# One transpose of a two-part staging tile becomes two, and the value matmuls take the high parts first

## The chip, the cores and the metric

The kernel runs on one core of one Trainium2 chip. The metric is the device time of one execution in microseconds. The engines are PE (matrix products; its weight loads are shown apart as PEld), DVE (vector), ACT (scalar), POOL (GpSimd) and SP (which here only issues DMA transfers).

## The reference, cut to what matters

A streaming-encoder block on x of 2048 rows by 1024 columns, float32. RMSNorm and one projection give the queries, keys and values of two kinds of heads; their outputs are normed, joined and projected back; a SwiGLU feed-forward part with a second RMSNorm follows. The change lies in the two attentions:

```python
# differential attention, 4 heads of value width 128, two softmax maps each
p = jax.nn.softmax(logits, axis=-1)
attn = p[:, :, 0] - lam * p[:, :, 1]
return jnp.einsum('bhqk,bkhd->bqhd', attn, v)
...
# stick-breaking attention, 8 heads of value width 64, strictly causal
log_1mb = jnp.where(mask, jax.nn.log_sigmoid(-z), 0.0)
rem = lax.cumsum(log_1mb, axis=3, reverse=True) - log_1mb
a = jnp.where(mask, jnp.exp(jax.nn.log_sigmoid(z) + rem), 0.0)
return jnp.einsum('bhqk,bkhd->bqhd', a, v)
```

Both are causal (the first by chunks of 64 rows), so a query block of 128 rows meets only the key blocks up to its own.

## The kernel before, in words

**Precision.** Every float32 operand of a matrix product is held as two float16 parts, a high one (the value rounded) and a low one (what is left). A product is made of three float16 products: high by high, high by low, low by high.

**Work and its order.** There are eight head groups g. Groups 0 to 3 hold one differential head each (`diff_attn`), groups 4 to 7 two stick-breaking heads each (`sb_attn`). While the attention of group g runs, the projection of group g+1 is woven in (`advance`, `proj_stream`), and out-projection work at the end. The feed-forward part comes after it all, from about 1360 us on. A scheduler of the framework places the instructions of each engine's queue at build time, by a timeline that it simulates and by priorities given in the code; the hardware then runs each queue strictly in that order, each instruction waiting for its semaphores.

**A unit of attention.** For a query block i (16 of them), a map or head m, and a stretch b of at most 1024 keys, the probabilities form a tile of 128 queries by n keys, n from 128 to 1024. In groups 0 to 3 the two maps are combined first, so that there are 24 units a group; in groups 4 to 7 there are 48. That makes 4 x 24 + 4 x 48 = 288 units. `split_t` (line 449) takes such a float32 tile and does three things:

- `to16` (line 454, instruction line 89 on ACT or DVE, 93 on POOL) casts it to the high part, in the first n columns of a staging tile s16. In stick-breaking heads ACT always does this.
- `tt` (line 455, instruction line 98) subtracts and writes the low part to the next n columns. In stick-breaking heads POOL always does this.
- `SP.dma_start_transpose` (line 460) turns all 2n columns, by DMA, into aT: up to 16 blocks of 128 keys by 128 queries, the high ones first.

The staging tile has three buffers and aT six (`SB`, `AB`, line 39); in groups 4 and 5 some units borrow buffers of the projection's tiles instead (lines 450 to 457). In a trace the staging tile is called `s`.

**Values.** `pv` (line 512) multiplies the n/128 blocks with the values and adds up in PSUM (yp): for each block j three matmuls, high aT by high v, high aT by low v, low aT by high v. In differential heads it runs two query blocks after the probabilities (`held`, line 584), in stick-breaking heads five or seven units after them (`lag`, line 599), and it may be placed only after the scores of the newest unit (line 632).

**SP's queue.** One queue issues nearly all transfers, in order: the transposes of line 460 and those of the queries and keys (line 409), copies of query halves (411), loads of normed rows for the projection (xt, 423), weights (271), stores of the attention's output (ms, 496). Each waits in the queue for its data, its buffer, and a completion semaphore out of eight that are used in turn.

Of the kernel before, what the change touches and what calls it, by code (L numbers as in the profile page):

```python
# [16 lines left out]
ALU = mybir.AluOpType  # L17
# [4 lines left out]
S, D, P = 2048, 1024, 128  # L22
# [37 lines left out]
def block(tc, a, out):  # L60
    nc = tc.nc
    PE, ACT, DVE, POOL, SP = nc.tensor, nc.scalar, nc.vector, nc.gpsimd, nc.sync
    top = ExitStack()
    with top:
# [11 lines left out]
        def pick(**cost):  # L76
            e = min(cost, key=lambda k: load[k] + cost[k] * KW[k])
            load[e] += cost[e] * KW[e]
            return e
# [5 lines left out]
        def to16(dst, src, n, engines="ADP", psum=False):  # L85
            cost = {"A": 0.84 * n + 110, "D": (1.05 if psum else 0.53) * n + 70, "P": 1.1 * n + 80}
            e = pick(**{k: cost[k] for k in engines})
            if e == "A":
                ACT.copy(dst, src)  # L89
            elif e == "D":  # L90
                DVE.tensor_copy(dst, src)
            else:
                POOL.tensor_scalar(dst, src, 1.0, 0.0, op0=ALU.mult, op1=ALU.add)

        def tt(dst, a_, b_, op, n, engines="DP"):
            cost = {"D": 1.15 * n + 70, "P": 2.45 * n + 80}
            e = pick(**{k: cost[k] for k in engines})
            (DVE if e == "D" else POOL).tensor_tensor(dst, a_, b_, op)  # L98

        def pri(k):  # L100
            def deco(f):
                @functools.wraps(f)
                def g(*args):
                    with tc.high_priority(PRI[k]) if PRI[k] else nullcontext():
                        return f(*args)
                return g
            return deco

        def nm(s):
            uid[0] += 1  # L110
            return f"{s}{uid[0]}"
# [144 lines left out]
        with ExitStack() as ph1:  # L256
# [75 lines left out]
            @pri("pm")  # L332
            def proj_turned(G, xt, pq, pv, r):
                xv = xt[:].rearrange("p (s k n) -> p s k n", s=2, k=KT)
                for c in range(3):
                    n = 0
                    for kt in range(KT):
                        for xi, wi in ((0, 0), (0, 1), (1, 0)):
                            w_, x_ = G["w"][:, wi, kt, 128 * c : 128 * c + 128], xv[:, xi, kt, :]
                            o = pv[:, P * r : P * r + P] if c == 2 else pq[:, 256 * c + P * r : 256 * c + P * r + P]  # L340
                            PE.matmul(o, lhsT=x_ if c == 2 else w_, rhs=w_ if c == 2 else x_, start=n == 0, stop=n == 23)  # L341
                            n += 1

            @pri("po")
            def turned_out(pq, pv, qT, kT, v, j):
                two = slice(j - 1, j + 1)
                q2, k2 = (pq[:, 256 * c : 256 * c + 256].rearrange("p (t n) -> p t n", t=2) for c in range(2))
                for m in range(2):
                    ACT.mul(qT[:, m, two, :], q2, half[:, m : m + 1])
                    DVE.scalar_tensor_tensor(qT[:, 2 + m, two, :], q2, half[:, m : m + 1], qT[:, m, two, :], op0=ALU.mult, op1=ALU.subtract)  # L350
                note("A", 800)
                note("D", 800)
                split_psum(kT[:, 0, two, :], kT[:, 1, two, :], k2, 256)
                vv = v[:, two, :].rearrange("p t (h s e) -> p t h s e", h=2, s=2)
                split_psum(vv[:, :, :, 0, :], vv[:, :, :, 1, :], pv[:, :256].rearrange("p (t h e) -> p t h e", t=2, h=2), 256)
# [92 lines left out]
            @pri("spl")  # L448
            def split_t(src, n, he="ADP", le="DP", wide=None):
                if wide is not None and wide % 5 in (1, 3):  # L450
                    s16 = pp.tile([P, 4, 256], F32, tag="raw", name=nm("s16"))[:].rearrange("p t n -> p (t n)").bitcast(F16)
                else:
                    s16 = s16p.tile([P, 2048], F16, tag="s16", bufs=SB, name=nm("s16"))
                to16(s16[:, :n], src, n, he)
                tt(s16[:, n : 2 * n], src, s16[:, :n], ALU.subtract, n, le)
                if wide is not None and wide % 4 == 3:
                    aT = pp.tile([P, 4, 4, 2, 64], F16, tag="st", name=nm("aT"))[:].rearrange("p c t s e -> p (c t) (s e)")
                else:
                    aT = sp.tile([P, 16, P], F16, tag="aT", bufs=AB, name=nm("aT"))
                SP.dma_start_transpose(aT[:, : 2 * n // P, :], s16[:, : 2 * n])  # L460
                return aT

            @pri("fin")
# [47 lines left out]
            @pri("pv")  # L511
            def pv(G, yp, y0, aT, b, n, o, wd, start, stop):
                nb = n // P
                for j in range(nb):
                    v = G["v"][2 * b + j // 4][:, j % 4, :]
                    for q, (a_, v_) in enumerate(((j, o), (j, o + wd), (nb + j, o))):
                        PE.matmul(yp[:, y0 : y0 + wd], lhsT=aT[:, a_, :], rhs=v[:, v_ : v_ + wd], start=start and j == 0 and q == 0, stop=stop and j == nb - 1 and q == 2, skip_group_check=True)  # L517

            def diff_attn(g, G):
                @pri("at")  # L520
                def probs(i):
# [43 lines left out]
                    for (b, n, z0), (_, _, z1) in zip(*zs):  # L565
                        DVE.scalar_tensor_tensor(z0[:, :n], z1[:, :n], rc[:], z0[:, :n], op0=ALU.mult, op1=ALU.add)
                        note("D", 1.05 * n + 130)
                        aTs.append((b, n, split_t(z0[:, :n], n)))
# [5 lines left out]
                def values(i, aTs, ssum):  # L574
                    r, k = fq(g, i)
                    if r == 0:
                        ypd[0] = ps.tile([P, 512], F32, tag="yp", name=nm("yp"))
                    yp = ypd[0]
                    for q, (b, n, aT) in enumerate(aTs):
                        pv(G, yp, P * r, aT, b, n, 0, 128, r == 0 and q == 0, r == k - 1 and q == len(aTs) - 1)  # L580
                    if r == k - 1:
                        finish(g, G, i, k, yp, ssum)
# [12 lines left out]
            def sb_attn(g, G):  # L595
# [5 lines left out]
                @pri("at")  # L601
                def stage_a(i, m, b):
                    L = (i + 1) * 128
                    n = min(1024, L - 1024 * b)
                    be, om = z4(), z4()
                    if b == i // 8:
                        DVE.memset(om[:, n : n + 1], 8192.0)
                    else:
                        DVE.tensor_copy(om[:, n : n + 1], last[m][:, 0:1])
                    last[m] = om  # L610
                    for c in range((n - 1) // 512, -1, -1):
                        lo, hi = 512 * c, min(512 * c + 512, n)
                        w = hi - lo
                        sc = ps.tile([P, 512], F32, tag="sc", bufs=4, name=nm("sc"))
                        front.append(score_chunk(G, sc, i, 2 * b + c, m, w // P, b == i // 8 and hi == n, turned(g)))
                        aside = c == 1 and turned(g)
                        beta = be[:, lo:hi] if aside else sc[:, :w]
                        ACT.activation(om[:, lo:hi], sc[:, :w], AF.Sigmoid, scale=G["nkz"][:])  # L618
                        ACT.activation(beta, sc[:, :w], AF.Sigmoid, scale=G["kz"][:])  # L619
                        ov = om[:, lo:hi][:, ::-1]  # L620
                        DVE.tensor_tensor_scan(ov, ov, sc[:, :w], om[:, hi : hi + 1], op0=ALU.mult, op1=ALU.bypass)  # L621
                        (POOL if aside else DVE).tensor_tensor(be[:, lo:hi], beta, om[:, lo + 1 : hi + 1], ALU.mult)  # L622
                        note("A", 1.7 * w + 400)
                        note("D", 2.1 * w + 150)
                        note("P" if aside else "D", (1.65 if aside else 1.05) * w + 100)
                    wide[0] += 1
                    return n, split_t(be[:, :n], n, "A", "P", wide[0] if g < NG - 2 else None)
# [670 lines left out]
```

## Time and profile before

| | us |
|---|---|
| median of 3 runs | 2703.69 |
| lowest and highest | 2701.29, 2709.12 |
| profiled execution | 2702.93 |
| its span (first to last instruction) | 2701.0 |

The profile is one execution. "Busy" counts an engine's own instructions; waiting, branching and issuing DMAs is the sequencer's and is not counted. A queue of an engine's sequencer is written with a q (SPq). A group's row gives the line, engine, operation, what is written <- what is read, the count, then busy us and mean ns of one, then the engine's idle time just before them and what ended it. A wait's row gives who waited for what: us in total, times, longest.

The attention with its projections takes the first half of the span, the feed-forward part the second:

| stage | about | what runs |
|---|---|---|
| differential heads | 100 to 600 us | groups 0 to 3, projections of 1 to 4 |
| stick-breaking heads | 600 to 1360 us | groups 4 to 7, projections of 5 to 7, out-projection |
| feed-forward | 1360 to 2701 us | nothing that the diff touches |

### The profile page before, as it was taken

To read this page: it belongs to the slowest core of one execution; us is meant where nothing else is said; L and a number is where in the kernel's file an instruction comes from. 1 tells how busy PE (TensorE), PEld (TensorE's weight loads), DVE (VectorE), ACT (ScalarE), POOL (GpSimd) and SP (SyncE) were. 2 spreads that over 40 slices of the span, in tenths; PEclk is the share of its full clock that TensorE was granted. 3 is DMA by queue.
4 is the path that set the end of the run, shared out by engine and by line. 5 is a ranking of instruction groups with operands and counts; after the bars stand their busy time and mean duration, and the time that the engine had idled before them with its cause. 6 is when DMAs were issued, how large, how long until landed. Compare 5 with 4: busy or idle time off the path is not lost. (4 is left out here: it accounts for less than half of the span.)

```text
span 2701.0 us, 50505 instructions
## 1 busy us (share of the span) xinstructions
PE 2508.6 (93%) x19628; PEld 1507.6 (56%) x19628; DVE 1959.8 (73%) x3712; ACT 1344.7 (50%) x2487; POOL 1517.8 (56%) x1097
## 2 busy tenths in 40 slices
PE   7998989899988989889999999999999999999999
PEld 4655656577776776567774444444444444444444
DVE  6898879899989889887866877778685543433434
ACT  4665656567978878765634534435352112111121
POOL 2578767768767767545665755665564332322323
PEclk9999999999999999999999999999999999999999
DMA  6778697768989989997996566565748744635532
GB/s 221 211 163 184 143 200 172 172 145 183 195 175 185 178 166 206 208 205 203 230 317 232 211 232 219 207 239 183 253 171 330 304 159 157 234 132 184 202 110 94
DMA packets 619584, 534.40 MB, mean 198 GB/s; under 512 B 480640, under 2 KB 548224, under 8 KB 609104
## 3 DMA queue, kind: packets, MB, share of 16 engines
q1 hardware_dynamic: 617520, 529.09, 70.1%
q8 instruction: 154, 2.52, 0.4%
q0 software_dynamic: 512, 1.36, 0.2%
q14 instruction: 86, 0.70, 0.1%
q10 hardware_dynamic: 1312, 0.72, 0.1%
HBM read 261.08 MB, written 147.32 MB: 151 GB/s over the span
## 5 line engine op out<-in xcount | busy, mean ns | idle before, releaser
L98 POOL TENSOR_TENSOR s<-z,s 128x1024 f16<-128x1024 f32 (+7 forms) x288 | 471.5, 1646 | 141.8 <-ACT s L89 118.2
L506 PE MATMUL sc<-kT,qT 128*128 128x512 f16 (+3 forms) x1520 | 382.7, 354 | 51.1 <-DVE z L622 18.6
L1104 PE MATMUL pd<-wd,act 128*128 128x512 f16 x1764 | 392.8, 380 | 5.3 <-DVE cu L1038 4.7
L621 DVE TENSOR_TENSOR_SCAN z<-z,sc 128x512 f32<-128x512 f32 (+3 forms) x320 | 352.8, 1112 | 56.5 <-ACT sc L619 34.6
L325 PE MATMUL pj<-w,xt 128*128 128x384 f16 x1920 | 354.6, 333 | 17.1 <-ACT raw L374 5.8
L1004 PEld LDWEIGHTS <-wu 128*128 128x128 f16 x1848 | 181.9, 98 | 224.6 <-issue 12.8
L1004 PEld LDWEIGHTS <-wg 128*128 128x128 f16 x1848 | 181.3, 98 | 222.9 <-issue 9.3
L517 PE MATMUL yp<-v,aT 128*128 128x64 f16 (+1 forms) x4896 | 271.2, 205 | 36.9 <-DMA aT<-s 35.7
L517 PEld LDWEIGHTS <-aT 128*128 128x128 f16 x4896 | 239.1, 100 | 114.4 <-DMA aT<-s 46.7
L98 POOL TENSOR_TENSOR act<-cg,act 128x512 f16<-128x512 f32 x109 | 150.7, 1393 | 259.4 <-ACT act L1063 259.4
L1104 PEld LDWEIGHTS <-act 128*128 128x128 f16 x1764 | 172.9, 98 | 213.5 <-issue 7.2
L325 PEld LDWEIGHTS <-xt 128*128 128x128 f16 x1920 | 187.8, 99 | 147.2 <-issue 23.4
L89 ACT CAST s<-z 128x128 f16<-128x128 f32 (+7 forms) x215 | 173.3, 810 | 135.9 <-DMA aT<-s 44.6
L98 POOL TENSOR_TENSOR stages<-stages 128x512 f32<-128x512 f32 x97 | 171.4, 1767 | 116.5 <-DVE wg L220 42.2
L618 ACT ACTIVATE z<-sc,c 128x512 f32<-128x512 f32 (+3 forms) x320 | 211.2, 665 | 24.4 <-PE sc L506 12.4
L98 POOL TENSOR_TENSOR hs<-hs,cu 128x512 f32<-128x512 f32 x102 | 133.6, 1317 | 159.3 <-DVE hs L1110 59.7
L506 PEld LDWEIGHTS <-qT 128*128 128x128 f16 x1520 | 128.8, 99 | 119.7 <-issue 23.9
L831 PE MATMUL po<-wo,mt 128*128 128x256 f16 x1536 | 182.4, 279 | 12.6 <-DVE xf L834 8.6
L1063 ACT CAST act<-cg 128x512 f16<-128x512 f32 x126 | 76.7, 616 | 231.1 <-DVE cg L1069 192.7
L1110 DVE SCALAR_TENSOR_TENSOR hs<-pd,c,hs 128x512 f32<-128x512 f32 x144 | 106.0, 747 | 115.0 <-PE pd L1104 105.3
L341 PE MATMUL pj<-xt,w 128*128 128x128 f16 x2304 | 177.4, 222 | 6.2 <-DVE v L363 5.2
L1004 PE MATMUL pm<-X,wu 128*128 128x512 f16 x792 | 179.8, 381 | 2.1 <-ACT cg L1049 1.7
(254 smaller groups left out, 4812.3 us busy)
## 6 DMA issues: line engine op xcount, KB each, us to landing
xt<-xs SPq DMA_DIRECT2D x112, 512.0 KB, 4.5
hs<-hd SPq DMA_DIRECT2D x72, 512.0 KB, 4.5
hd<-hs SPq DMA_DIRECT2D x56, 512.0 KB, 5.9
split<-wg SPq DMA_DIRECT2D x11, 1792.0 KB, 6.9
split<-wu SPq DMA_DIRECT2D x11, 1792.0 KB, 6.7
split<-wd SPq DMA_DIRECT2D x11, 1792.0 KB, 6.8
wg<-split SPq DMA_DIRECT2D x11, 1792.0 KB, 7.5
wd<-split SPq DMA_DIRECT2D x11, 1792.0 KB, 9.0
```

The source lines that it names most:

```text
L89: ACT.copy(dst, src)
L98: (DVE if e == "D" else POOL).tensor_tensor(dst, a_, b_, op)
L325: PE.matmul(pj[:, :384], lhsT=xv[:, xi, kt, :], rhs=G["w"][:, wi, kt, :], start=n == 0, stop=n == 23)
L341: PE.matmul(o, lhsT=x_ if c == 2 else w_, rhs=w_ if c == 2 else x_, start=n == 0, stop=n == 23)
L506: last = PE.matmul(sc[:, : 128 * w].rearrange("p (t n) -> p t n", n=P), lhsT=G["q"][i // 4][:, a_, i % 4, :], rhs=G["k"][q][:, b_, 0:w, :] ...
L517: PE.matmul(yp[:, y0 : y0 + wd], lhsT=aT[:, a_, :], rhs=v[:, v_ : v_ + wd], start=start and j == 0 and q == 0, stop=stop and j == nb - 1 a ...
L618: ACT.activation(om[:, lo:hi], sc[:, :w], AF.Sigmoid, scale=G["nkz"][:])
L621: DVE.tensor_tensor_scan(ov, ov, sc[:, :w], om[:, hi : hi + 1], op0=ALU.mult, op1=ALU.bypass)
L831: PE.matmul(po[:, sl], lhsT=mt[:, kt, P * xi : P * xi + P], rhs=wos[2 * h + n][wi][:, kt, :], start=q == 0, stop=q == 23)
L1004: PE.matmul(ps_[:].rearrange("p (t n) -> p t n", n=P), lhsT=wv[:, wo, wi, 128 * kt : 128 * kt + 128], rhs=X[xo][:, :, xi, kt, :], start=st ...
L1104: PE.matmul(po[:], lhsT=act[:, ao, xi, 128 * j : 128 * j + 128], rhs=W["d"][:, wo, wi, :], start=start and u == 0 and q == 0, stop=u == nu ...
L1110: DVE.scalar_tensor_tensor(dst, po[:], kd[:], src, op0=ALU.mult, op1=ALU.add)
```

## The change

In `split_t` aT is taken ahead of the cast, and the single transpose of 2n columns becomes two of n columns: the high part's right after the cast, the low part's after the subtraction. In `pv` the order of the 3n/128 matmuls of a unit changes: all blocks' high-aT pairs first, then all low-aT ones. Numbers of matmuls, casts and subtractions, their shapes and the bytes moved stay the same; there are 288 more DMA transposes.

```diff
-                to16(s16[:, :n], src, n, he)
-                tt(s16[:, n : 2 * n], src, s16[:, :n], ALU.subtract, n, le)
                 if wide is not None and wide % 4 == 3:
                     aT = pp.tile([P, 4, 4, 2, 64], F16, tag="st", name=nm("aT"))[:].rearrange("p c t s e -> p (c t) (s e)")
                 else:
                     aT = sp.tile([P, 16, P], F16, tag="aT", bufs=AB, name=nm("aT"))
-                SP.dma_start_transpose(aT[:, : 2 * n // P, :], s16[:, : 2 * n])
+                to16(s16[:, :n], src, n, he)
+                SP.dma_start_transpose(aT[:, : n // P, :], s16[:, :n])
+                tt(s16[:, n : 2 * n], src, s16[:, :n], ALU.subtract, n, le)
+                SP.dma_start_transpose(aT[:, n // P : 2 * n // P, :], s16[:, n : 2 * n])
                 return aT
...
             def pv(G, yp, y0, aT, b, n, o, wd, start, stop):
                 nb = n // P
-                for j in range(nb):
+                todo = [(j, a_, v_) for part in (((0, o), (0, o + wd)), ((nb, o),)) for j in range(nb) for a_, v_ in part]
+                for q, (j, a_, v_) in enumerate(todo):
                     v = G["v"][2 * b + j // 4][:, j % 4, :]
-                    for q, (a_, v_) in enumerate(((j, o), (j, o + wd), (nb + j, o))):
-                        PE.matmul(yp[:, y0 : y0 + wd], lhsT=aT[:, a_, :], rhs=v[:, v_ : v_ + wd], start=start and j == 0 and q == 0, stop=stop and j == nb - 1 and q == 2, skip_group_check=True)
+                    PE.matmul(yp[:, y0 : y0 + wd], lhsT=aT[:, a_ + j, :], rhs=v[:, v_ : v_ + wd], start=start and q == 0, stop=stop and q == 3 * nb - 1, skip_group_check=True)
```

## The prediction

> **What bounds the kernel now.** I read the page's busy shares first, then the stretches of the attention stage, then the DMA-issuing queue SP, because the change touches only how the staging tiles of attention are transposed. The page:
>
> ```profile
> PE 2508.6 (93%) x19628; PEld 1507.6 (56%) x19628; DVE 1959.8 (73%) x3712; ACT 1344.7 (50%) x2487; POOL 1517.8 (56%) x1097
> ...
> L517 PE MATMUL yp<-v,aT 128*128 128x64 f16 (+1 forms) x4896 | 271.2, 205 | 36.9 <-DMA aT<-s 35.7
> L517 PEld LDWEIGHTS <-aT 128*128 128x128 f16 x4896 | 239.1, 100 | 114.4 <-DMA aT<-s 46.7
> ```
>
> PE is busy for 93% of the span, and the matmuls that the change reorders (line 517) leave it idle for 36.9 us in all, 35.7 of them until a transposed tile aT lands. PEld shows the same waits from the weight load's side, so the two are not added. Where the attention runs, the stretches (start:end, length, then busy time of PE, PEld, DVE, ACT, POOL, granted clock, DMA share, GB/s) say:
>
> ```profile
> 100.00:600.00 500.00, 456.58 (x3861) 302.41 (x3860) 433.48 (x1284) 302.40 (x791) 351.87 (x252) 0.97 0.76 171
> 600.00:800.00 200.00, 179.93 (x2765) 147.81 (x2763) 181.08 (x336) 167.05 (x318) 147.89 (x114) 0.98 0.94 186
> 800.00:1100.00 300.00, 267.20 (x3858) 205.62 (x3857) 271.58 (x470) 245.40 (x441) 215.38 (x157) 0.98 0.93 187
> ...
> 1200.00:1360.00 160.00, 147.67 (x1599) 124.62 (x1597) 122.92 (x183) 97.61 (x163) 101.68 (x67) 0.98 0.84 214
> ```
>
> From 100 to 600 us (differential heads) PE leads and the DMA engines have a quarter of their time free. From 600 to 1100 (stick-breaking heads) PE 90%, DVE 90%, ACT 83% and the DMA engines 93 to 94% are all nearly full: no engine has room there. After 1360 us nothing of the change runs; the 1340 us of the feed-forward part stay as they are.
>
> The transposes, as the view of line 460 gives them (ns in the SP queue min/median/max; then issue to landing), with the subtraction ahead of them from the view of the staging tile:
>
> ```profile
> L460 SPq DMA_TRANSPOSE aT<-s x288: 1167/1556/5872, 113.7 to 1358.9; - x144
> DMA to landing us min/median/max: 2.3/3.9/7.9
> ```
> ```profile
> L98 POOL TENSOR_TENSOR s<-z,s x288: 416/1890/3642, 112.9 to 1356.1; 128x1024 f16<-128x1024 f32 x70, 128x128 f16<-128x128 f32 x12, 128x640 f16<-128x640 f32 x12, 128x896 f16<-128x896 f32 x12
> ```
>
> One transpose holds SP's in-order queue for at least 1.17 us, whatever its size; ordinary transfers hold it far less (0.53 us for an xt load in the rows below). 288 at the median are 288 x 1.56 = 449 us of SP's time between 114 and 1359 us.
>
> **The change part by part.** Matmuls and weight loads: 4896 of each before and after, the same operands, so no price in PE time. Each aT block still serves two matmuls in a row, then one. ACT, DVE and POOL run the same casts and subtractions. The same bytes are moved.
>
> *Issues.* SP issues 288 transposes more. A half has one to eight 128-column blocks. The small end is the first unit of the attention (two blocks), in SP's timeline; the large end has a row of its own, since the transposes of qT and kT (line 409) are just eight blocks:
>
> ```profile
> 113.67 1.20 SPq L460 DMA_TRANSPOSE aT<-s  x1
> ...
> 118.93 0.53 SPq L423 DMA_DIRECT2D xt<-xs  x1
> ```
> ```profile
> L409 SPq DMA_TRANSPOSE qT<-st x20: 1231/1258/2072, 71.9 to 1177.2; - x20
> L409 SPq DMA_TRANSPOSE kT<-st x20: 1232/1298/3267, 74.0 to 1178.4; - x20
> ...
> DMA to landing us min/median/max: 3.1/3.3/6.6
> ```
>
> So a half costs 1.20 to 1.26 us of SP, a pair 2.40 to 2.52 us. 288 more issues at 1.2 us are 346 us of SP's time. The Trainium skill, "DMA: Bandwidth & Descriptors", section on the anatomy of one DMA, puts nearly all of a DMA's fixed cost of about 2 us (measured there for GpSimd's queue) into the completion and about 50 ns into the sequencer's dispatch; by that the 288 issues would be an estimated 14 us of SP. The trace's 1.17 us minimum, on SP's queue and for a transpose, speaks against it here.
>
> *What covers them.* SP's own waits ahead of line 460 (us in total, times, longest):
>
> ```profile
> SPq L460 <- POOL s L98: 299.3, 123, 11.6
> ...
> SPq L460 <- POOL z L622: 97.4, 39, 9.1
> ...
> SPq L460 <- POOL raw L98: 24.1, 6, 7.3
> ...
> SPq L460 <- POOL s L93: 20.1, 10, 3.8
> ...
> SPq L460 <- POOL yrs L485: 15.4, 8, 3.4
> ```
>
> For 123+39+6+10+8 = 186 of the 288 units SP sat idle, 456 us in all, until GpSimd had ended the low half or what stands just ahead of it. There the high half's issue falls into the wait and costs nothing, as it was meant. About 102 units had no such wait; SP was behind already. Two stretches of SP's timeline show these bursts:
>
> ```profile
> 620.96 15.98 SPq L460 DMA_TRANSPOSE aT<-s  x10
> ...
> 666.99 18.38 SPq L460 DMA_TRANSPOSE aT<-s  x8
> ```
>
> Ten units took 1.60 us each with nothing between them, mostly small ones at the start of a head; eight took 2.30 us each, half of them sixteen blocks long, in a stretch where the DMA engines are 94% busy, so that SP probably waited for room in them. As pairs they take 2.40 to 2.52 us: 0.8 us more a unit in the first kind, 0.2 us in the second. Over 102 units that is 20 to 82 us by which SP falls further behind; I take the middle, 50 us.
>
> *Who waits for that.* SP is one queue. Behind a low half that waits for GpSimd stand the next unit's high half, the xt loads of the projection and the stores of ms; in the built order the two halves of a unit mostly stand side by side, so the high half of unit n+1 cannot pass the low half of unit n. A late landing reaches PE (which runs seven units behind the scores, so some is absorbed) and ACT (which needs the staging buffer back; there are three, and two shared ones in two groups). Whole span, then from 600 to 1200 us:
>
> ```profile
> ACT s L89 <- DMA aT<-s: 44.6, 23, 4.3
> ...
> PE yp L517 <- DMA aT<-s: 35.7, 27, 3.3
> ```
> ```profile
> PE yp L517 <- DMA aT<-s: 13.2, 13, 2.1
> ```
> ```profile
> ACT s L89 <- DMA aT<-s: 24.3, 17, 3.0
> ```
>
> Both engines wait on these landings already, in the stretch in which neither has room, so lateness is not free. I let half of the 50 us through, 25 us (bounds: nothing, and all 82). The high half also needs its aT buffer about 1.9 us (the median subtraction) sooner; with six buffers I price that at nothing, and where a buffer is late it is part of the same lateness, at most 1.9 us a time.
>
> *What is gained.* The last landing of a unit is now that of eight blocks or fewer: 3.3 us after its issue instead of 3.9, so 0.6 us sooner where SP is on time. Outside 600 to 1200 us PE waits 27-13 = 14 times, 22.5 us: 14 x 0.6 = 8 us saved. Inside, SP's lateness eats it.
>
> *Order.* The built program places the value matmuls earlier: at the 128th unit 339 fewer projection matmuls stand ahead of them than before, over units 96 to 192 about 50 to 120. PE passes 2765 matmuls in the 200 us from 600 on, 0.072 us each, so up to 24 us of filler work comes later exactly where SP and the DMA engines are full. The work itself is not lost; I take nothing, and 24 us for the upper end.
>
> *Sum.* 25 - 8 = 17, about +18 us with the rounding of the halves. The profiled execution lasted 2702.9 us (span 2701.0), 0.8 below the median of 2703.7. So 2721 on the profile's own time and **2722** as a median, 0.7% slower.
>
> **The rivals.** Line 460 once more, from 600 to 800 us and from 800 to 1100 us (first row of one, both rows of the other):
>
> ```profile
> L460 SPq DMA_TRANSPOSE aT<-s x66: 1190/1559/5872, 601.0 to 799.7; - x66
> ```
> ```profile
> L460 SPq DMA_TRANSPOSE aT<-s x84: 1167/1630/5492, 799.7 to 1097.4; - x84
> DMA to landing us min/median/max: 2.3/4.5/7.9
> ```
>
> *Halves land earlier, and SP keeps up (faster).* For it: 186 units with an idle SP ahead of them, and a DMA queue with a quarter of its time free before 600 us. Against it: SP's 1.2 us a piece. If SP's lateness stays hidden, each of PE's 27 waits shrinks by 0.6 us (all rows) to 1.2 us (if a full unit's landing of about 4.5 us becomes 3.3): 16 to 32 us, 2672 to 2688, middle 2680. It holds as long as a pair is issued faster than units are made: a unit takes 200 us / 66 = 3.0 us from 600 to 800, a pair 2.5 us and the other transfers some 0.3 (an xt load of 0.53 us to two units). The Trainium skill's rule on dispatch would give this outcome.
> *No change.* From 600 to 1100 us the DMA engines are 93% busy with the same bytes; if they set the pace, the split is hidden and gain and lateness cancel: 2696 to 2711.
> *The split does not do what it says (far slower).* If a high half regularly queues behind a low half that waits for GpSimd, nothing starts earlier and each unit has 1.2 us more of latency, while xt loads stand in the same line. Then all 82 us of lateness come through with the 24 of the order: 2703.7 + 106, about 2810. It decides once the pair plus other transfers (2.8 us) exceeds the unit's 3.0 us by any extra wait of 0.2 us.
>
> **How the numbers follow.** Forecast, moderately slower (2712, where no change ends, to 2778, when all 82 us of lateness come through less the 8 gained): 0.50. Faster: 0.27. No change: 0.15. Far slower: 0.08. A measurement of this kernel tells about 0.3% (8 us) from no change, so faster 0.27, same 0.15, slower 0.58. The range runs from 2672, the low end of the faster rival, to 2778; only the far-slower rival is outside, and some of the tails. The likeliest case alone spans 2712 to 2778.
>
> **What would show it.** SP's view of the two transpose lines should have 288 rows each with minima near 1.17 us and medians of 1.25 to 1.5 us. In bursts, SP's timeline should show pairs at 2.4 to 2.5 us with no gap. The forecast is right if PE's and ACT's waits on aT between 600 and 1200 us grow from 13.2 and 24.3 us to some 20 to 30 more in sum, and PE's waits before 600 us shrink. It is wrong, towards faster, if those waits fall everywhere while SP's waits for GpSimd shrink by about 300 us; wrong towards far slower if xt loads start to hold up PE's projections (lines 325 and 341). A much shorter issue for a half (0.6 us, half of now) would take away the ground of the whole forecast.

## The result and the profile after

The changed kernel takes 2829.99 us (median of 4 runs, 2828.66 to 2834.37) against 2702.49 us: ratio 1.047, 95% interval 1.0456 to 1.0484. It is 127 us slower. The forecast had the sign and was far too small; the time lies above its whole range.

The profiled execution has a span of 2832.5 us. Its page, with the rows that answer to those of before:

```profile
PE 2531.9 (89%) x19628; PEld 1519.7 (54%) x19628; DVE 1960.2 (69%) x3712; ACT 1349.1 (48%) x2487; POOL 1514.8 (53%) x1097
...
L518 PE MATMUL yp<-v,aT 128*128 128x64 f16 (+1 forms) x4896 | 286.8, 206 | 84.2 <-DMA aT<-s 83.8
L518 PEld LDWEIGHTS <-aT 128*128 128x128 f16 x4896 | 248.0, 101 | 164.0 <-DMA aT<-s 103.5
```

The engines do the same work in a longer time: DVE's busy time is 1960 us as before, at 69% of the span and no longer 73%. PE's idle time ahead of the value matmuls went from 36.9 to 84.2 us, and its busy time from 2508.6 to 2531.9 us for the same matmuls; its mean granted clock was 0.967 and no longer 0.98. The stretches (busy time of PE, PEld, DVE, ACT, POOL, granted clock, DMA share, GB/s) show where:

```profile
100.00:600.00 500.00, 435.76 (x3509) 284.00 (x3508) 398.90 (x1197) 285.16 (x744) 333.22 (x238) 0.96 0.74 162
600.00:800.00 200.00, 154.14 (x2105) 121.10 (x2104) 161.86 (x330) 143.71 (x280) 129.34 (x97) 0.93 0.77 154
800.00:1100.00 300.00, 251.71 (x3940) 207.83 (x3939) 239.00 (x422) 215.26 (x395) 185.38 (x142) 0.97 0.84 157
```

From 100 to 600 us PE gets through 3509 matmuls instead of 3861, from 600 to 800 through 2105 instead of 2765. Every engine has room there, and so have the DMA engines, 77% and no longer 94%: everybody waits. The two transposes of a unit (ns in SP's queue, first and last start, landing):

```profile
L459 SPq DMA_TRANSPOSE aT<-s x288: 1103/1236/3911, 114.5 to 1475.3; - x144
...
DMA to landing us min/median/max: 2.3/3.3/10.3
```
```profile
L461 SPq DMA_TRANSPOSE aT<-s x288: 1093/1237/3547, 117.3 to 1479.1; - x144
...
DMA to landing us min/median/max: 2.2/3.0/9.3
```

Each half holds SP for 1.24 us at the median, as forecast. The last one starts at 1479 us; the last transpose of before started at 1359. The two profiled executions differ by 131 us, so 120 of these were lost ahead of that point, in the attention. Some 12 us come behind the last value matmul: 1348 us from there to the end against 1336 before. SP's queue in a stretch of the attention:

```profile
759.33 1.30 SPq L461 DMA_TRANSPOSE aT<-s  x1
760.73 1.27 SPq L459 DMA_TRANSPOSE aT<-s  x1
762.10 1.27 SPq L461 DMA_TRANSPOSE aT<-s  x1
763.47 1.22 SPq L459 DMA_TRANSPOSE aT<-s  x1
...
787.28 2.62 SPq L423 DMA_DIRECT2D xt<-xs  x3
```

In the first rows issue follows issue at 0.1 us, and the three xt loads stand behind them. A stretch of the same queue before has gaps of 1.3 and 2.0 us between the end of one row and the start of the next:

```profile
719.91 0.32 SPq L423 DMA_DIRECT2D xt<-xs  x1
720.32 1.53 SPq L460 DMA_TRANSPOSE aT<-s  x1
723.19 0.32 SPq L423 DMA_DIRECT2D xt<-xs  x1
725.52 9.60 SPq L460 DMA_TRANSPOSE aT<-s  x4
```

Over the whole attention 85 of the 288 transposes of before had a gap of at least 1.2 us ahead of them; in the changed kernel 35 of the 576 have one.

PE's own account, from 100 us to about the last value matmul (same columns as above, first the kernel before, then the changed one):

```profile
100.00:1360.00 1260.00, 1133.51 (x12869) 835.66 (x12868) 1089.67 (x2435) 877.93 (x1843) 862.72 (x624) 0.97 0.85 185
```
```profile
100.00:1480.00 1380.00, 1162.93 (x12897) 851.42 (x12895) 1085.64 (x2435) 883.49 (x1846) 864.73 (x625) 0.95 0.80 169
```

Of the 120 us PE spends 91 idle (217 us and no longer 126) and 29 on nearly the same matmuls at a lower granted clock. Its waits grew from 35.7 to 83.8 us for aT, from 9.7 to 42.5 us for all other transfers, which stand in SP's queue too, and from 71 to 83 us for DVE. How much of the 29 us would be lost without the waits, no run shows.

### The profile page after: what moved, and what is told of

It reads as the page before. It is cut to its first block, busy times and chain, and to the rows that moved or that the text cites. A ratio compares the mean times of both kernels' runs of the same rounds, so it can differ in the third digit from the quotient of the medians.

```text
span 2832.5 us, 51199 instructions
## 1 busy us (share of the span) xinstructions
PE 2531.9 (89%) x19628; PEld 1519.7 (54%) x19628; DVE 1960.2 (69%) x3712; ACT 1349.1 (48%) x2487; POOL 1514.8 (53%) x1097
## 5 line engine op out<-in xcount | busy, mean ns | idle before, releaser
L98 POOL TENSOR_TENSOR s<-z,s 128x1024 f16<-128x1024 f32 (+7 forms) x288 | 461.5, 1609 | 204.3 <-ACT s L89 195.4
L518 PE MATMUL yp<-v,aT 128*128 128x64 f16 (+1 forms) x4896 | 286.8, 206 | 84.2 <-DMA aT<-s 83.8
L518 PEld LDWEIGHTS <-aT 128*128 128x128 f16 x4896 | 248.0, 101 | 164.0 <-DMA aT<-s 103.5
L619 ACT ACTIVATE z<-sc,c 128x512 f32<-128x512 f32 (+3 forms) x320 | 208.4, 655 | 59.1 <-PE sc L509 42.5
L543 DVE TENSOR_SCALAR_CACHE_REDUCE z<-sc,c 128x512 f32<-128x512 f32 (+3 forms) x256 | 162.3, 648 | 44.3 <-PE sc L507 40.0
```

Source lines behind the costliest of these rows:

```text
L518: PE.matmul(yp[:, y0 : y0 + wd], lhsT=aT[:, a_ + j, :], rhs=v[:, v_ : v_ + wd], start=start and q == 0, stop=stop and q == 3 * nb - 1, ski ...
L543: DVE.tensor_scalar(z[:, lo : lo + f], sc[:, :f], kz_d[:], None, op0=ALU.mult, op1=ALU.max, accum_out=mx[:, m, nx : nx + 1])
```

## The experiments

Two things change on the chip: SP issues 288 transposes more (theory A), and the scheduler, which sees other dependencies, puts the instructions of all engines into another order (theory B). To part them, most kernels below have their queues fixed: an ordering edge, which orders issue and makes nobody wait for completion, ties every instruction to the one ahead of it in a given order.

```python
for a_, b_ in zip(at, at[1:]):          # at: the positions of one engine's queue in the given order
    tc.add_manual_dep(ins[b_], ins[a_].name, dep, reason="order")
```

"Old order" is the queue order of the kernel before, "new order" that of the changed kernel. The kernel before gave 2703 to 2705 us beside these runs.

**1. The change in the old order** (`split_old_order`): the changed kernel plus the edges.

> The changed kernel's instructions (two transposes a unit, the high half right after the cast, high blocks first in the values), but every engine's queue is fixed to the order that the kernel before has, with the two transposes side by side where the one stood. Theory A (SP's queue: 288 more issues of about 1.2 us in a queue that runs in order) expects nearly the whole loss without the scheduler's new order: 2780 to 2830 us. Theory B (the scheduler, which takes the halves to be cheaper, built an order that the hardware cannot keep) expects 2690 to 2720 us. If both take part, something between.

2780.0 us, ratio 1.028 (1.0268 to 1.0301): 77 us slower, the lower end of what theory A expected. The extra issues cost that in the order of before; the new matmul order, which is in this kernel too, costs nothing (trial 7). SP's timeline shows the backlog: high (459) and low halves (461) without a gap.

```profile
716.26 1.66 SPq L461 DMA_TRANSPOSE aT<-s  x1
718.01 0.53 SPq L423 DMA_DIRECT2D xt<-xs  x1
718.63 1.18 SPq L459 DMA_TRANSPOSE aT<-s  x1
719.90 1.21 SPq L461 DMA_TRANSPOSE aT<-s  x1
```

Summed over all its transfers between 600 and 1200 us, SP is issuing for 87% of the time; before it was 66%. Who pays, from 600 to 1200 us (us in total, times, longest):

```profile
PE yp L518 <- DMA aT<-s: 44.7, 49, 5.3
```
```profile
ACT s L89 <- DMA aT<-s: 66.6, 33, 7.2
```

Before these were 13.2 and 24.3 us. ACT's wait is the longer: its cast waits for a staging buffer that the late transpose has not read yet. The wait runs from the queue back to the producer.

**2. One transpose in the new order** (`one_new_order`): the kernel before with the new values' order, and edges for the new order.

> One transpose a unit as before, but every engine's queue is fixed to the order of the changed kernel, high blocks first in the values; the one transpose stands where the high half stood. Theory A expects the time of before or some 10 us more, 2695 to 2715 us, since 288 issues are gone. Theory B expects most of the loss, 2780 to 2830 us. The place at the high half makes SP wait for the subtraction there, so a result between is no clean verdict.

2855.1 us, ratio 1.056 (1.0545 to 1.0576). Slower than the change itself, with half its transposes. This does not measure the order cleanly: the values' high matmuls stand early in that order, and here they wait for a transpose that needs both halves (PE waits 97.8 us for aT over the span; 83.8 in the changed kernel). Trial 9 mends most of it.

**3. Both halves issued late, old order** (`split_late_old_order`):

```diff
-                SP.dma_start_transpose(aT[:, : n // P, :], s16[:, :n])
                 tt(s16[:, n : 2 * n], src, s16[:, :n], ALU.subtract, n, le)
+                SP.dma_start_transpose(aT[:, : n // P, :], s16[:, :n])
```

> As the changed kernel in the order of before, but both halves' transposes are issued only after the subtraction, so nothing starts early. If the early high half is worth what it was meant to be (about 2 us of latency a unit), this is 10 to 40 us slower than the same with the early half; if SP's issue time alone counts, within 10 us of it; if a high half that waits in the queue blocks others, this is faster by 5 us or more.

2780.9 us against 2780.0 of trial 1. But the edit did not bring what the expectation says. The subtraction writes other columns than the high half's transpose reads, so neither waits for the other, and the place of a line in the code is not its place in a fixed queue. In the two traces SP's queue holds the same operations in the same order, and PE's too, and in both some 60 of the 288 high halves start before their unit's subtraction has ended. So this is a repeat of trial 1; what the early start is worth it does not show.

**4. The values' order alone, scheduler free** (`pv_only`): the hunk of `pv` without that of `split_t`.

> One transpose a unit as before; only the value matmuls take all high blocks first; the scheduler is free. Theory A expects no change beyond the scheduler's own scatter, 2690 to 2715 us. A theory that the new matmul order itself costs time (theory C) expects 2760 us or more.

2729.8 us, ratio 1.0094 (1.0077 to 1.0111): 27 us, for the same instructions and transfers. Neither theory had expected that: it lies above the range of A and below that of C.

**5. Split only where SP had a gap, old order** (`split_idle_old_order`): here and in 6, 8, 10 and 12 the values keep their old matmul order.

```diff
+                two = next(seen) in TWO
+                if two:
+                    SP.dma_start_transpose(aT[:, : n // P, :], s16[:, :n])
                 tt(s16[:, n : 2 * n], src, s16[:, :n], ALU.subtract, n, le)
+                f = n if two else 0
+                SP.dma_start_transpose(aT[:, f // P : 2 * n // P, :], s16[:, f : 2 * n])
```

> Queues fixed to the order of before, values in the old matmul order; only those 85 units are split before which SP's queue had been empty for at least 1.2 us in the trace of before (the gap between the end of one issue and the start of the next). Theory A (an extra issue costs only where SP has no gap) expects 2690 to 2712 us. If every extra issue costs the same, 77 us / 288 = 0.27 us each, it gives 2726 us.

2702.9 us beside 2704.9, ratio 0.9992 (0.9982 to 1.0002). 85 issues more, free, and no gain clear of noise either: at the lower end of the interval 5 us. Here 83 of the 85 high halves do start before their subtraction has ended, by 1.8 us at the median. This is as near as any variant came to beating the kernel before.

**6. The complement, old order** (`split_busy_old_order`): `TWO` holds the other 203 units.

> The complement: the other 203 units are split, those where SP was busy or nearly so. Theory A expects nearly the whole loss of the fixed order, 2760 to 2785 us. Equal cost for each issue gives 2703 + 203 x 0.27 = 2757 us. If the units with gaps were what holds up the queue, it stays below 2730 us.

2776.1 us, ratio 1.0267 (1.0247 to 1.0287): 71 us, 0.35 us for each of these units. The same kernel with all 288 units split is trial 8, 81 us slower. So most of the loss sits in these units, and the cost depends on where the issue falls. Whether the other 85 are still free once these 203 are split is not shown: 10 us lie between the two trials, and their intervals just overlap.

**7. The values' order alone, old order** (`pv_old_order`).

> One transpose a unit, values with all high blocks first, every queue fixed to the order of before. If the 27 us of the values' order alone came from the scheduler's new order, this is 2700 to 2710 us. If the matmul order itself costs PE time, it is 2720 to 2735 us.

2702.6 us, ratio 1.0001 (0.9985 to 1.0018). So the 27 us of trial 4 are the scheduler's order alone; the new matmul order costs nothing.

**8. The split alone, old order** (`split_only_old_order`): trial 1 without the hunk of `pv`.

> Two transposes a unit, values in the old matmul order (each block's high and low part side by side, so the first block needs both halves), queues fixed to the order of before. If taking high blocks first lets PE start earlier to any use, this is slower than 2780 us by 10 us or more; if the matmul order does not matter, 2775 to 2785 us.

2785.9 us, ratio 1.0304 (1.0277 to 1.033). Trial 1 gave 2780.0 beside a slightly faster kernel before (77 us slower against 81), so taking the high blocks first is worth some 4 us if anything; the two intervals overlap.

**9. One transpose in the new order, at the low half's place** (`one_new_order_low`).

> A fairer trial of the changed kernel's order without its extra issues: queues fixed to the order of the changed kernel, one transpose a unit, standing at the low half's place for 234 units (the other 54 at the high half's place, where the low place would close a circle of waits), and the values of a unit all together at the place of its first low block. If the loss beyond the 77 us of the issues comes from the order, this is 2740 us or more; if the order is harmless and the trial before it was slow for its odd places, 2695 to 2715 us.

2813.2 us, ratio 1.0411 (1.0395 to 1.0428): 110 us slower with as many transposes as before. Its stretches look like those of the change:

```profile
100.00:600.00 500.00, 436.18 (x3563) 286.73 (x3561) 397.54 (x1199) 288.06 (x752) 337.53 (x240) 0.95 0.71 163
600.00:800.00 200.00, 163.10 (x2186) 127.27 (x2184) 171.90 (x342) 151.76 (x290) 137.08 (x102) 0.91 0.74 158
```

PE again passes only 3563 and 2186 matmuls, and no engine nor the DMA engines are full. PE's waits from 600 to 1200 us:

```profile
PE yp L517 <- DMA aT<-s: 17.7, 9, 4.4
PE sc L506 <- DVE z L621: 15.5, 16, 5.1
PE pj L341 <- DVE v L363: 13.2, 6, 4.1
PE sc L506 <- DVE z L622: 9.6, 14, 1.5
```

Here PE waits less for transposes than for DVE to free the scores' and projections' buffers. Over the whole attention its waits for DVE grew from 71 us before to 105, those for aT from 36 to 56. That the queues' orders fit each other less well is the likely reading, not a shown one. 54 of the 288 transposes stand at a place of their own, so the 110 us have a share of that in them.

**10. Three transposes a unit, old order** (`three_old_order`): trial 8 with the low half cut once more.

```diff
-                SP.dma_start_transpose(aT[:, n // P : 2 * n // P, :], s16[:, n : 2 * n])
+                f = n + n // P // 2 * P
+                if f > n:
+                    SP.dma_start_transpose(aT[:, n // P : f // P, :], s16[:, n:f])
+                SP.dma_start_transpose(aT[:, f // P : 2 * n // P, :], s16[:, f : 2 * n])
```

> The suspected cost doubled: queues fixed to the order of before, values in the old matmul order, and three transposes a unit (the low half is cut once more; the 24 units of one block keep two), 264 issues more than with two. With three, SP needs 552 x 1.2 + 288 x 1.2 = 1010 us for these transposes and some 230 us for the rest, about the whole attention stage of 1260 us of before, so theory A expects it to be the bound throughout: each further issue costs nearly its full 1.2 us, 2780 + 264 x 0.8 to 1.2 = 2990 to 3100 us. If the loss with two came from contention of the DMA engines or the order of work, it stays below 2850 us.

2996.4 us, ratio 1.1087 (1.1066 to 1.1109). Against the 2785.9 of trial 8 that is 210.5 us for 264 issues, 0.80 us each: more than twice the 0.27 to 0.35 us of the second issue. The dose is steep because the cover is used up: SP is issuing for 91% of the time from 600 to 1200 us, and its gaps ahead of these transposes sum to 90 us (127 in trial 8, 292 before). The DMA engines meanwhile have more and more room:

```profile
600.00:800.00 200.00, 150.16 (x1897) 118.08 (x1896) 141.03 (x334) 115.57 (x246) 110.89 (x84) 0.90 0.61 127
```

At a DMA share of 0.61 it is not the transfer itself that is late but its issue. The Trainium skill's "DMA: Bandwidth & Descriptors", section on the anatomy of one DMA, gives about 50 ns for a dispatch, on GpSimd's path; by that, 264 issues would be an estimated 264 x 0.05 = 13 us. The measurement decides for the 1.2 us of SP's rows.

**11. The change with late issue, scheduler free** (`split_late_free`): the diff of trial 3, without edges.

> The changed kernel with both transposes issued after the subtraction, scheduler free. The issues cost about 77 us with a fixed order; the scheduler's order is free to add or take away some 50 us, as it did in the changed kernel (127 in all) and with the values' order alone (27). 2760 to 2850 us. At or below 2780 us the early high half is what led the scheduler to the bad order; near 2830 us it is not.

2828.4 us, the change's own time. As in trial 3, the edit does not make the issue late: 184 of the 288 high halves start before their subtraction has ended, against 185 in the changed kernel. The scheduler built another order from it, which costs as much; whether the early issue led it there stays open.

**12. Split only where SP had a gap, scheduler free** (`split_idle_free`): trial 5 without edges.

> Only the 85 units with a gap in SP's queue are split, values in the old matmul order, scheduler free. With the fixed order this cost nothing (2703 us). Whatever it differs from 2703 us now is the scheduler's order alone: theory B's scatter expects 2690 to 2760 us, anything but equal; if the order mattered only where issues are many, 2698 to 2708 us.

2740.4 us, ratio 1.014 (1.0125 to 1.0155). The same instructions take 2702.9 us in the old order. So 37 us come from the order alone; in the old order these issues cost nothing.

## Why the prediction was wrong

Right: the sign, the issue time of a half (1.20 to 1.26 us forecast, 1.24 measured), the place (SP's queue in the attention), and no price for the matmuls' order (trial 7). The sign that the forecast named also came: PE's and ACT's waits on aT between 600 and 1200 us grew from 37.5 to 58.4 us in sum, by 21 us of the 20 to 30. That the loss was 127 us and not 18 shows how little of it these two waits catch. PE's waits on aT before 600 us did not shrink, they grew from 20.6 to 42.4 us. Lateness that comes back through the staging buffer to ACT shows in trial 1 (24.3 to 66.6 us), hardly in the changed kernel (27.4 us). Wrong were four terms of the sum, all in one direction.

- **The cover.** "186 of the 288 units SP sat idle, 456 us in all". That was read from SP's view of waits, in which rows of line 460 sum to 502 us. Over all rows of SP's timeline of before, the gaps between the end of one issue and the start of the next transpose sum to 292 us. 135 gaps exceed 0.15 us, and only 85 reach the 1.2 us that an extra issue needs. The view's totals include time in which the issue already ran. Trials 5 and 6 then showed that those 85 are free on their own and that the other 203 carry most of the cost; the forecast had 102.
- **Half let through.** "I let half of the 50 us through". In the old order 77 us came through. The forecast's own prices for 203 units in place of 102 give 41 to 162 us of lateness, half of the middle 51 us; so the share let through was too low as well, unless the price of a unit was. The runs do not part these two. What they show is that the transposes took 841 us of SP's time in trial 1 and 546 before, 295 us more, of which 77 reached the end.
- **The gain.** "14 x 0.6 = 8 us saved". Outside 600 to 1200 us, where it was to be saved, PE's waits on aT grew from 22.5 to 52.8 us. In trial 5, with 85 units split and hardly any time lost by it, at most 5 us were gained, and none clear of noise.
- **The order.** "The work itself is not lost; I take nothing". This is the step that failed most in kind. The forecast saw that the value matmuls move ahead of up to 339 projection matmuls, and priced it at 0 to 24 us. The same instructions take 50 us more in the new order than in the old one (2830 against 2780, trial 1). One transpose a unit in nearly that order costs 110 us (trial 9), and two edits that cost nothing themselves cost 27 and 37 us by their orders (trials 4 and 12).

The two profiled executions behind the 50 us differ by 57. Of these, 27 are lost up to the last value matmul of the differential heads, 18 more up to the last of the stick-breaking heads, and 12 behind it, where the forecast said that nothing changes (the kernels in the old order differ by up to 7 us there). PE idles 33 us more than in trial 1 up to the last value matmul, and its matmuls take 13 us more.

With 77 for the issues and 50 for the order the sum closes by construction; the two are not independent, for 77 + 110 is more than 127. A likely reason is that the new order was made for two landings a unit, and trial 9 gives it one. That was only argued. Open also is what in the new order costs most: no run gives one engine the new order and the others the old one. Nor does a run split the transposes without the new values' order under a free scheduler.

Of the rivals, "far slower" (2810 us, chance 0.08) came nearest in time, and part of its mechanism is there: behind SP's backlog the xt loads hold up the projections, which cost PE 2.7 us in the whole span before. From 600 to 1200 us in the changed kernel:

```profile
PE yp L518 <- DMA aT<-s: 31.0, 25, 3.6
PE sc L507 <- DVE z L622: 16.5, 20, 5.1
PE pj L341 <- DMA xt<-xs: 14.6, 5, 7.6
```

But that nothing starts earlier did not come true: 185 of the 288 high halves start before their subtraction has ended, by 1.6 us at the median, and the kernel is slow all the same. The rival that SP keeps up falls with trials 1 and 6. "No change" falls with the DMA shares: the DMA engines did not set the pace, they got emptier.

No variant beats the kernel before. The experiments point to fewer issues in SP's busy stretches, which no edit here tried.

## What to carry to other kernels

Count the issues of an in-order DMA queue as work of an engine, here some 1.2 us a piece from one block to eight, and search its timeline for gaps, one by one, since a sum of waits says nothing of how many fit. A second, smaller transfer was free here where a gap of its issue time stood ahead of it, and cost 0.35 us of its 1.2 us where none did; a third cost 0.8 us. Where a scheduler places the instructions, its new order is part of every edit and can cost as much as the edit; fix the old order to see the edit alone. And see in the trace that an edit does what it was meant to do: moving a line of code moved no transpose in trial 3.

## What the runs showed of the hardware that was not expected

A transpose of a single 128-column block holds SP almost as long as one of eight: 1.18 against 1.26 us at the median in the changed kernel, where the shortest of all is 1.09 us. It is not the same at every size: before, the transposes of sixteen blocks held SP for 2.08 us at the median. Why, no run shows. Halving the transfer shortened its landing by little, from 3.9 to 3.3 and 3.0 us.

The granted clock of TensorE was lower in the kernels in which PE waited more: 0.98 over the span before, 0.967 in the changed kernel, 0.945 with three transposes, and 0.90 from 600 to 800 us in that last one. With it the same matmuls took longer: PE's busy time up to the last value matmul was 1216 us before, 1239 in the changed kernel and 1306 with three transposes. So by the profile, part of PE's longer time is slower matmuls and not waiting. What sets the granted clock was not tried.
